# Four S5 pairs side by side: the lag matrices of a hybrid trunk in four column quarters of TensorE

## The chip, the cores and the metric

The kernel runs on one core of one Trainium2 chip. The metric is device time in microseconds (us). Three runs of the kernel before gave 1427.63, 1430.24 and 1431.34 us, median 1430.24.

A core has five engines that work side by side, each through its own list of instructions in order: TensorE (PE in the profile, its weight loads apart as PEld), VectorE (DVE), ScalarE (ACT), GpSimd (POOL) and SyncE (SP). They wait for each other by semaphores. DMAs are issued from the lists of SP, ACT and POOL. A TensorE product holds one operand still (the weights, up to 128 rows by 128 columns) and moves the other through; the columns of the weights become the partitions of the result, in an accumulator (PSUM). What takes a product of fp32 operands is two records in the trace.

## The reference

Four layers over 256 time steps of width 1024, all fp32. Each adds a mixer, an MLP and an embedding gate to `h`; the mixer of layers 0 and 3 is S5, a diagonal complex state-space layer over 64 groups of 16 channels with 64 states each:

```
def s5_mixer(xn, w_in, lam_re, lam_im, log_dt, b_re, b_im, c_re, c_im, d_skip, w_glu, w_out):
    u = (xn @ w_in).astype(f32)
    dt = jnp.exp(log_dt.astype(f32))[:, None]
    mag = jnp.exp(lr * dt)
    ab_re, ab_im = mag * jnp.cos(li * dt), mag * jnp.sin(li * dt)
    ...
    bbar_re = coef_re[..., None] * br - coef_im[..., None] * bi
    bbar_im = coef_re[..., None] * bi + coef_im[..., None] * br
    ...
        x_re = jnp.einsum('bsgc,gnc->bsgn', u_blk, bbar_re)
        x_im = jnp.einsum('bsgc,gnc->bsgn', u_blk, bbar_im)
        pa_re, pa_im, s_re, s_im = lax.associative_scan(_cplx_combine, (a_re, a_im, x_re, x_im), axis=1)
    ...
        y = jnp.einsum('bsgn,gcn->bsgc', s_re, cr) - jnp.einsum('bsgn,gcn->bsgc', s_im, ci)
    ...
    y = y.swapaxes(0, 1).reshape(bsz, t, D_MODEL) + d_skip.astype(f32) * u
    z = jax.nn.gelu(y).astype(xn.dtype) @ w_glu
    z1, z2 = jnp.split(z, 2, axis=-1)
    return (z1 * jax.nn.sigmoid(z2)) @ w_out

def reference(...):
    for i in range(DEPTH):                       # mixers: S5, FoX, GLA, S5
        h = h + mixer(rmsnorm(h, norm_mix[i]))
        h = h + sqrelu_mlp(rmsnorm(h, norm_mlp[i]), mlp_w1[i], mlp_w2[i])
        gate = jax.nn.sigmoid(rmsnorm(h, norm_ple[i]) @ ple_gate[i])
        h = h + (p[i] @ ple_proj[i]) * gate
    return rmsnorm(h, final_norm)
```

FoX (layer 1) is an attention with forget gates, GLA (layer 2) a gated linear attention.

## The kernel before

**Dense products.** Weights come from HBM in units of 512 KB (`raw`) on SP's queue. ACT rounds each unit (L179, `whi`), DVE makes the rest (L181, `wlo`), and TensorE multiplies high by high, high by low and low by high (L198 to L200, or in wider pieces L234 and L236). The stages outside S5 are almost wholly such products.

**S5 in steps of four.** Time is cut into 64 chunks of four steps. For the 64 steps of the chunk index a scan carries the state; within a chunk of four an input acts on an output 0 to 3 steps later by a small matrix of 16 by 16 channels, the lag matrix (the skip `d` is added to lag 0). The 64 groups go in 32 pairs, and the pairs in four blocks `b` of eight. For a block:

- `U` (L984): the block's inputs, loaded from DRAM by eight DMAs, alternately on ACT and SP.
- the way in, `s5_way_in` (L996): `U` times `wh`/`wl` (the matrices B with their powers) into `wk`, 64 products.
- rotation, scan and turning back on DVE (L908 to L911, L1006 to L1011, L1021 to L1025), which give `R`, `P` and `W`.
- `s5_way_out` (L926 to L938): `qo` (C with the powers of the state matrix, DVE) and `bx` (B masked by group, ACT).
- `s5_inside` (L942 to L954), the lag matrices. For each pair and each of real and imaginary part one product: weights `bx`, 128 rows by 32 columns (two groups of 16 channels); moving `qo`, 64 columns (four lags by 16 channels). The result of a block, `pk`, is 32 partitions by 8 pairs by 64. It stands in one accumulator bank (tag `mk`, one buffer), which an opening product with zeros (L946) sets up; a closing product of the identity with `dd` (`d` on the diagonals, L951) adds the skip. ACT copies it to `kk` (L953).
- `s5_lags` (L956 to L964): four DMAs (L961) write `kk` into `tm`, 128 partitions (32 channels by four input steps), shifted by 16 columns for each step, so that `tm` holds all lags of a chunk. In layer 0 they go from `kk` on ACT and SP, two on each.
- `s5_outputs` (L1042): `U` times `tm`, then `P` and `W` times `qo`, into a bank of the same tag `mk`; Gelu (L1051); transposition (L1058).

**Layer 3 is prepared ahead.** What of S5 does not depend on `h` is made for layer 3 by a generator, `s5_ahead`, whose steps are put between the dense products of earlier layers: `win`, `rot`, `qo` and `kk` of each block are stored in DRAM (`kept`; `kk` in slot 3) by DMAs on POOL, and read back in layer 3 on POOL's queue, `kk` by four shifted DMAs into `tm`. So of layer 3's four lag blocks only the reading stands in layer 3; their products stand in dense stages.

**What sets the order.** In layer 0 a string of steps (a letter and a block) gives the order in which the program is written:

```
FIRST = """i0 w2 w3 r0 x0 f2 w4 o0 j2 P0 s0 k0 w5 u1 w6 d0 e0 y0 r1 i1 f3 x1 t0 o1 j3 k1 g0 u2 w7 l0 P1 d1 s1 a0 p0 e1 y1 r2 i2 x2 t1 o2 k2 g1 ...
```

(`w` in-projection, `u` loads of `U`, `x` way in, `o` way out, `k` lag products, `s` and `e` scan and turning, `y` outputs, `t` and `g` transposition and split, `d` and `l` loads and splits of the next weights, `a` and `b` gate products, `p` embedding product.) A scheduler then orders each engine's list by its own estimate of times, and gives semaphores and buffers; it may move an instruction past others of its engine. A change of an instruction's kind can thus move others.

## Time and profile before

| | us |
|---|---|
| three runs, median | 1430.24 |
| profiled execution, span from first to last instruction | 1426.6 |
| PE busy in it | 1396.1 |
| PE weight loads (beside PE) | 1258.1 |
| DVE busy | 1034.8 |
| ACT busy | 710.6 |
| POOL busy | 100.6 |
| mean DMA rate | 178 GB/s |

The profile gives of the profiled execution no time but its span; the median of the three runs is 3.6 us above it. A line such as

```profile
L949 PE MATMUL mk<-qo,bx x256: 219/219/311, 37.6 to 1046.2; 128*32 128x64 f32 x128
```

reads: line 949 of the program, on PE, result `mk` from `qo` (moving) and `bx` (weights), 256 records, the shortest, median and longest in ns, the first and last start in us; then weights 128 rows by 32 columns and 128 partitions by 64 moving elements. The ends of matmuls are modelled and overlap the next one's start, so what a product costs is read from start to start. "idle before <-" names the time in which the engine had nothing to do before an instruction and what it waited for. The granted clock, 1.00 where nothing is throttled, was 0.996 in the mean.

Of the eight lag blocks four lie in layer 0 (at 37.6, 61.3, 80 to 86 and 110.7 us of the span) and four in dense stages, ahead for layer 3 (at 606, 892, 951 and 1042 us).

### The profile page before, as it was taken

The page shows a single profiled execution, that of the slowest core. Times are in us where ns is not written, and L with a number is a line of the kernel's source. Part 1 is how long each engine was busy: PE and PEld are TensorE (multiplying, and loading weights), DVE is VectorE, ACT ScalarE, POOL GpSimd, SP SyncE. Part 2 cuts the span into 40 slices and gives each one's busy share as a digit, 9 for nine tenths or more (in the row PEclk, how much of TensorE's full clock was granted, in tenths as well). Part 3 has the DMA queues.
Part 4 walks back from the last instruction along what each step waited for, and adds up shares of the span by engine and source line. Part 5 has one row for each costly group of instructions (what it writes and reads, how often), then busy time and mean ns, then how long its engine had stood idle before and what let it go on. Part 6 is the DMA issues. An engine that isn't in the chain of part 4 may idle for free.

```text
span 1426.6 us, 26530 instructions
## 1 busy us (share of the span) xinstructions
PE 1396.1 (98%) x10754; PEld 1258.1 (88%) x10754; DVE 1034.8 (73%) x1636; ACT 710.6 (50%) x1110; POOL 100.6 (7%) x167
## 2 busy tenths in 40 slices
PE   9999999999999999999999999999999999999997
PEld 8889988889999888889989588888998899888897
DVE  9985678776866678897676468878656946766765
ACT  3234465454655665455567445445552345545543
POOL 3000000010110000100005000000003100000020
PEclk9999999999999999999999999999999999999999
DMA  9443556657554355866565445667656556556661
GB/s 299 113 121 110 184 170 196 190 180 237 178 150 137 120 167 186 270 210 201 193 181 152 133 129 183 207 195 221 201 188 196 185 183 179 178 176 205 187 184 60
DMA packets 143227, 254.54 MB, mean 178 GB/s; under 512 B 21648, under 2 KB 32240, under 8 KB 143104
## 3 DMA queue, kind: packets, MB, share of 16 engines
q1 hardware_dynamic: 129856, 227.66, 51.8%
q0 software_dynamic: 7360, 23.73, 4.8%
q10 hardware_dynamic: 5888, 1.44, 0.5%
q8 instruction: 84, 1.38, 0.4%
q14 instruction: 39, 0.32, 0.1%
HBM read 242.15 MB, written 7.86 MB: 175 GB/s over the span
## 4 chain that ended last, share of the span: by engine, by line
PE 66%; DVE 1%; ACT 1%; issue 1%; DMA 0%; DVEq 0%; POOLq 0%; ACTq 0%
PE wk L234 9%; PE acc L234 7%; PE wk L236 4%; PE wk L198 4%; PE wk L200 4%; PE wk L199 4%; PE acc L236 4%; PE acc L198 3%; PE acc L199 3%; PE acc L200 3%; PE mk L234 3%; PE po L234 2%; PE acc L1150 1%; PE mk L236 1%; PE acc L259 1%; PE acc L258 1%
## 5 line engine op out<-in xcount | busy, mean ns | idle before, releaser
L181 DVE TENSOR_TENSOR wlo<-raw,whi 128x1024 fp32r<-128x1024 f32 x396 | 482.2, 1226 | 278.3 <-ACT whi L179 275.6
L179 ACT CAST whi<-raw 128x1024 fp32r<-128x1024 f32 x396 | 412.2, 1049 | 461.2 <-DMA raw<-mlp_w 69.1
L234 PE MATMUL wk<-x,whi 128*128 128x512 f32 x576 | 181.3, 396 | 1.1 <-DVE relu L245 1.1
L236 PEld LDWEIGHTS wk<-x,wlo 128*128 128x128 f32 x576 | 106.8, 188 | 23.4
L234 PE MATMUL acc<-s,whi 128*128 128x512 f32 x384 | 119.2, 395 | 0.0
L236 PE MATMUL wk<-x,wlo 128*128 128x256 f32 x576 | 112.9, 279 | 0.0
L234 PEld LDWEIGHTS wk<-x,whi 128*128 128x128 f32 x576 | 90.3, 189 | 3.6 <-DVE relu L245 1.4
L236 PEld LDWEIGHTS acc<-s,wlo 128*128 128x128 f32 x384 | 71.0, 188 | 16.1
L198 PE MATMUL acc<-x,whi 128*128 128x256 f32 x288 | 81.7, 287 | 0.8 <-ACT pp L432 0.8
L200 PE MATMUL acc<-x,wlo 128*128 128x256 f32 x288 | 82.2, 286 | 0.2 <-DVE wlo L181 0.2
L199 PE MATMUL acc<-x,whi 128*128 128x256 f32 x288 | 81.8, 285 | 0.0
L234 PE MATMUL mk<-x,whi 128*128 128x512 f32 x256 | 81.7, 396 | 0.0
L236 PE MATMUL acc<-s,wlo 128*128 128x256 f32 x384 | 75.4, 280 | 0.0
L200 PE MATMUL wk<-s,wlo 128*128 128x256 f32 x256 | 72.4, 283 | 0.0
L199 PE MATMUL wk<-s,whi 128*128 128x256 f32 x256 | 72.4, 283 | 0.0
L198 PE MATMUL wk<-s,whi 128*128 128x256 f32 x256 | 72.4, 283 | 0.0
L234 PE MATMUL po<-s,whi 128*128 128x512 f32 x192 | 60.3, 395 | 0.0
L234 PEld LDWEIGHTS acc<-s,whi 128*128 128x128 f32 x384 | 59.1, 188 | 0.9
L234 PE MATMUL wk<-s,whi 128*128 128x512 f32 x192 | 59.1, 395 | 0.0
L234 PE MATMUL acc<-x,whi 128*128 128x512 f32 x192 | 58.8, 396 | 0.0
L236 PEld LDWEIGHTS mk<-x,wlo 128*128 128x128 f32 x256 | 47.6, 188 | 10.3
L198 PEld LDWEIGHTS acc<-x,whi 128*128 128x128 f32 x288 | 54.8, 191 | 2.1 <-ACT pp L432 1.3
(405 smaller groups left out, 3405.7 us busy)
## 6 DMA issues: line engine op xcount, KB each, us to landing
raw<-mlp_w SPq DMA_DIRECT2D x256, 512.0 KB, 4.1
raw<-s_w_glu SPq DMA_DIRECT2D x32, 512.0 KB, 4.1
raw<-ple_gate SPq DMA_DIRECT2D x32, 512.0 KB, 3.8
raw<-fox_w_in SPq DMA_DIRECT2D x24, 512.0 KB, 3.9
raw<-gla_w_in SPq DMA_DIRECT2D x24, 512.0 KB, 4.4
raw<-s_w_out SPq DMA_DIRECT2D x16, 512.0 KB, 3.7
kept<-kept POOLq DMA_DIRECT2D x12, 512.0 KB, 5.6
raw<-ple_proj SPq DMA_DIRECT2D x8, 512.0 KB
```

Of the source, the lines that this page charges most:

```text
L179: nc.scalar.copy(hi, raw)
L181: self.last_lo = nc.vector.tensor_tensor(lo, raw, hi.bitcast(F32), ALU.subtract)
L198: mm(ps, hi, x[:, 0], start=first, stop=False, skip_group_check=True)
L199: mm(ps, hi, x[:, 1], start=False, stop=False, skip_group_check=True)
L200: self.last_mm = mm(ps, lo, x[:, 0], start=False, stop=last, skip_group_check=True)
L234: mm(ps[n], hi[:, i, s], v[i], start=first and i == 0, stop=False, skip_group_check=True)
L236: self.last_mm = mm(ps[n][:, 0], lo[:, i, s], v[i][:, 0], start=False, stop=last and i == UK - 1, skip_group_check=True)
L258: mm(ps[half], a[:, 0, t], hi[:, k], start=k0 + k == 0, stop=False)
L259: mm(ps[half], a[:, 0, t], lo[:, k], start=False, stop=False)
L1150: self.last_mm = nc.tensor.matmul(ps[:, n], raw[:, k, c], x[4 * i + k], start=i == k == n == 0, stop=i == 1 and k == 3, skip_group_check=True)
```

## The change

The sixteen products of a block keep their size, but are laid out in four column quarters: pair `p = 2 r + h` goes to columns 32 r to 32 r + 31, so to partitions 32 r to 32 r + 31 of the result, which is now 128 partitions by two pairs by 64. The four quarters follow each other in the order of the program; the first product of each quarter opens it (`start`), and the product with zeros is gone. The skip is added by four products of the identity, 32 columns each, one for each quarter; `dd` becomes 128 by 8 by 16 for 32 by 32 by 16, and for it `eye16` gets 128 rows (three additions for one) and the skip's table another layout, made on the host. `kk` is 128 by 128 for 32 by 512.

`s5_lags` wants the eight pairs of a channel in one partition. So `kk` now goes to DRAM first, by four DMAs, one a quarter: in layer 0 into a new `lags`, alternately on ACT and SP, and from there by the four shifted DMAs into `tm`; for layer 3 into `kept` as before, by four DMAs on POOL for one.

```diff
--- before.py
+++ after.py
@@ -99,8 +99,11 @@
         nc.gpsimd.affine_select(self.blk[:, 1:2], self.ones[:, :1], [[0, 1]], ALU.is_ge, 0.0, base=-64, channel_multiplier=1)
         self.nblk = const("nblk", [P, 2])
         nc.scalar.mul(self.nblk, self.blk, -1.0)
-        self.eye16 = const("eye16", [32, 16])
-        nc.vector.tensor_tensor(self.eye16, self.ident[0:32, 0:16], self.ident[0:32, 16:32], ALU.add)
+        self.eye16 = const("eye16", [P, 16])
+        eyes = const("eyes", [P, 64])
+        nc.vector.tensor_tensor(eyes, self.ident[:, 0:64], self.ident[:, 64:128], ALU.add)
+        nc.vector.tensor_tensor(eyes[:, 0:32], eyes[:, 0:32], eyes[:, 32:64], ALU.add)
+        nc.vector.tensor_tensor(self.eye16, eyes[:, 0:16], eyes[:, 16:32], ALU.add)
         self.zero = const("zero", [1, 512], BF16)
         nc.gpsimd.memset(self.zero, 0.0)
         self.halfpi = const("halfpi", [P, 1])
@@ -715,7 +718,7 @@
         lam = self.lam if self.lam is not None else self.s5_load(j)
         self.lam = None
         lr, li, ld = (lam[:, i, :] for i in range(3))
-        sd = self.small("sd", [32, 32], bufs=1)
+        sd = self.small("sd", [128, 8], bufs=1)
         (nc.sync if late else nc.gpsimd).dma_start(sd, self.A["s5_dT"][j])
         new = lambda name: self.small(name, [128, 32], bufs=1)
         tt = V.tensor_tensor
@@ -818,8 +821,8 @@
         cmul(at(F8, 3, 5), at(F8, 1, 3), rep(F8, 2, 2), 32, 2)
         yield
         cmul(at(F8, 5, 8), at(F8, 1, 4), rep(F8, 4, 3), 32, 3)
-        d = self.small("dd", [32, 32, 16], bufs=1)
-        self.tc.keep_in_program_order(V.tensor_tensor(d, self.eye16.unsqueeze(1).broadcast_to([32, 32, 16]), sd.unsqueeze(2).broadcast_to([32, 32, 16]), ALU.mult))
+        d = self.small("dd", [128, 8, 16], bufs=1)
+        self.tc.keep_in_program_order(V.tensor_tensor(d, self.eye16.unsqueeze(1).broadcast_to([128, 8, 16]), sd.unsqueeze(2).broadcast_to([128, 8, 16]), ALU.mult))
         r4 = new("r4")
         tt(r4, mag, mag, ALU.mult)
         tt(r4, r4, r4, ALU.mult)
@@ -936,22 +939,31 @@
         for g in range(2):
             nc.scalar.activation(bx[:, 0, :, g, :], bc[:, 0], AF.Identity, scale=self.blk[:, g:g + 1])
             nc.scalar.activation(bx[:, 1, :, g, :], bc[:, 1], AF.Identity, scale=self.nblk[:, g:g + 1])
-        dd = q["d"][:, ps]
+        dd = q["d"][:, 2 * b:2 * b + 2]
         return out, qo, bx, dd
 
     def s5_inside(self, b, out, qo, bx, dd, ahead=False):
 
         nc = self.nc
-        pk = self.psum((32, 8, 4, 16), "mk")
-        nc.tensor.matmul(pk, self.zero[:, 0:32], self.zero, start=True, stop=False, skip_group_check=True)
-        for p in range(8):
+        pk = self.psum((128, 2, 4, 16), "mk")
+        rows = [slice(32 * r, 32 * r + 32) for r in range(4)]
+        for h in range(2):
             for i in range(2):
-                nc.tensor.matmul(pk[:, p], bx[:, i, p].rearrange("x g c -> x (g c)"), qo[i][:, 0:4, p, :],
-                                 start=False, stop=False, skip_group_check=True)
-        nc.tensor.matmul(pk[:, :, 0, :], self.ident[0:32, 0:32], dd, start=False, stop=True, skip_group_check=True)
-        kk = self.t2("kk", (32, 8, 4, 16))
-        nc.scalar.copy(kk, pk)
-        return out, self.keep(b, 3, kk, ahead) if ahead else self.s5_lags(b, kk.rearrange("x p l c -> x p (l c)"), (nc.scalar, nc.sync))
+                for r in range(4):
+                    p = 2 * r + h
+                    nc.tensor.matmul(pk[rows[r], h], bx[:, i, p].rearrange("x g c -> x (g c)"), qo[i][:, 0:4, p, :],
+                                     start=h == i == 0, stop=False, skip_group_check=True)
+        for r in range(4):
+            nc.tensor.matmul(pk[rows[r], :, 0, :], self.ident[rows[r], rows[r]], dd[rows[r]], start=False, stop=True, skip_group_check=True)
+        kk = self.t2("kk", (128, 2, 64))
+        nc.scalar.copy(kk, pk.rearrange("x h l c -> x h (l c)"))
+        if not ahead and b == 0:
+            self.lags = self.dram.tile([4, 32, 512], F32, name="lags")
+        to = self.kept[0][b, 3, 0:32, 0:512] if ahead else self.lags[b]
+        for r in range(4):
+            queue = nc.gpsimd if ahead else (nc.scalar, nc.sync)[r % 2]
+            queue.dma_start(to[:, r * 128:(r + 1) * 128], kk[rows[r]].rearrange("x h e -> x (h e)"))
+        return out, kk if ahead else self.s5_lags(b, to.rearrange("x (p f) -> x p f", p=8), (nc.scalar, nc.sync))
 
     def s5_lags(self, b, kk, queues):
 
@@ -1418,7 +1430,7 @@
     o["s5_lam"] = np.stack([state(a["s5_lam_re"]), state(a["s5_lam_im"]), state(ldt)], axis=2)
     b = lambda v: v.reshape(n, 4, 8, 2, 64, 16).transpose(0, 3, 4, 1, 2, 5).reshape(n, 128, 4, 8, 16)
     c = lambda v: v.reshape(n, 4, 8, 2, 16, 64).transpose(0, 3, 5, 1, 2, 4).reshape(n, 128, 4, 8, 16)
-    o["s5_dT"] = a["s5_d"].reshape(n, 32, 32).transpose(0, 2, 1)
+    o["s5_dT"] = a["s5_d"].reshape(n, 4, 4, 2, 32).transpose(0, 2, 4, 1, 3).reshape(n, 128, 8)
 
     bT = lambda v: np.broadcast_to(v.reshape(n, 4, 8, 2, 64, 16).transpose(0, 1, 3, 5, 2, 4)[:, :, :, :, None], (n, 4, 2, 16, 4, 8, 64)).reshape(n, 4, 128, 512)
     o["s5_bT"] = np.stack([bT(a["s5_b_re"]), bT(a["s5_b_im"])], axis=3)
```

The names of lines below are those of each program (the change moves them by 3 to 12).

**ACT's list, around the lag matrix of block 1 in layer 0** (`kk` is the copied result, `U` the next block's inputs, `tm_...` the lag matrices, `whi` a rounded weight unit). Before:

```order
L953 COPY kk<-mk 32x512
L179 CAST whi<-raw 128x1024
L961 DMA tm_109<-kk 32x512
L961 DMA tm_109<-kk 32x8x32
L984 DMA U<-u 128x1x64 x4
```

Now:

```order
L959 COPY kk<-mk 128x128
L965 DMA lags<-kk 32x128 x2
L996 DMA U<-u 128x1x64
L973 DMA tm_112<-lags 32x512
L973 DMA tm_112<-lags 32x8x32
L996 DMA U<-u 128x1x64 x3
```

The rounding of a weight unit has moved ahead, out of this place; two writes to `lags` have come in, and three of the four `U` loads stand behind the reads into `tm`, one ahead of them. On SP the loads of `U` are parted in the same way, and three weight loads now stand ahead of that block's writes.

**PE's list, around the outputs of block 0 in layer 0** (`U` with `tm_...`, then `P` and `W`, are the outputs; `wk<-U` is the way in of block 1). Before:

```order
L1150 MATMUL acc<-x,wh 128x256 x7
L1042 MATMUL mk<-tm_108,U 64x64 x16
L1042 MATMUL mk<-qo,P 64x64 x32
L1042 MATMUL mk<-qo,W 64x64 x32
L996 MATMUL wk<-U,wh 64x64 x2
```

Now:

```order
L1162 MATMUL acc<-x,wh 128x256 x8
L1054 MATMUL mk<-tm_111,U 64x64 x16
L1008 MATMUL wk<-U,wh 64x64 x2
L1008 MATMUL wk<-U,wl 64x64 x2
L1008 MATMUL wk<-U,wh 64x64 x2
L1008 MATMUL wk<-U,wl 64x64 x2
L1008 MATMUL wk<-U,wh 64x64 x2
L1008 MATMUL wk<-U,wl 64x64
L1054 MATMUL mk<-qo,P 64x64 x32
L1054 MATMUL mk<-qo,W 64x64 x32
L1008 MATMUL wk<-U,wl 64x64
```

Eleven way-in products of block 1 have moved ahead of the products with `P`. In the next block, 24 of block 2's 64 way-in products have moved ahead of the products with `tm`.

**DVE's list, around `qo` of block 2 in layer 0** (`qo` and `scratch` are the two halves of a complex product, which the subtraction and the addition of `qo<-qo,scratch` join, here with the numbers that tell block 2's (1085, now 1101) from block 3's (1429, now 1451); `wlo` is the rest of a weight unit; `F` are powers). Before:

```order
L911 TENSOR_TENSOR rot_999<-rot_999,scratch_1000 128x8x64
L926 TENSOR_TENSOR scratch_1086<-bc_550,cpow_252 128x1280
L181 TENSOR_TENSOR wlo_1316<-raw_1154,whi_1315 128x1024
L926 TENSOR_TENSOR qo_1429<-bc_814,cpow_252 128x1280
L929 TENSOR_TENSOR qo_1085<-qo_1085,scratch_1086 128x640
L930 TENSOR_TENSOR qo_1085<-qo_1085,scratch_1086 128x640
L908 TENSOR_TENSOR scratch_1344<-F1_312,F8_313 128x1024
```

Now:

```order
L914 TENSOR_TENSOR rot_1015<-rot_1015,scratch_1016 128x8x64
L184 TENSOR_TENSOR wlo_1338<-raw_1176,whi_1337 128x1024
L929 TENSOR_TENSOR scratch_1102<-bc_553,cpow_255 128x1280
L932 TENSOR_TENSOR qo_1101<-qo_1101,scratch_1102 128x640
L933 TENSOR_TENSOR qo_1101<-qo_1101,scratch_1102 128x640
L911 TENSOR_TENSOR scratch_1366<-F1_315,F8_316 128x1024
L929 TENSOR_TENSOR qo_1451<-bc_824,cpow_255 128x1280
```

The rest of the weight unit stands ahead of the multiplication into `scratch`, and block 3's multiplication has moved behind the two joins.

## The prediction

> **What bounds the kernel now.** I read the page's busy shares first, then the chain of waits, then busy time by stretch.
>
> ```profile
> span 1426.6 us, 26530 instructions
> PE 1396.1 (98%) x10754; PEld 1258.1 (88%) x10754; DVE 1034.8 (73%) x1636; ACT 710.6 (50%) x1110; POOL 100.6 (7%) x167
> PE 66%; DVE 1%; ACT 1%; issue 1%; DMA 0%; DVEq 0%; POOLq 0%; ACTq 0%
> ```
>
> PE is busy 98% of the span and makes nearly all of the chain that is named. A microsecond of TensorE work saved is a microsecond of time where PE runs without a gap, and is nothing where it then waits. So the stretch decides:
>
> ```profile
> 28.00:55.00 27.00, 24.99 (x330) 21.82 (x330) 26.77 (x32) 5.26 (x12) 4.21 (x8) 1.00 0.62 179
> 55.00:80.00 25.00, 23.67 (x564) 21.95 (x560) 18.97 (x22) 8.50 (x16) 0.54 (x1) 1.00 0.27 73
> 80.00:100.00 20.00, 17.76 (x164) 15.59 (x165) 18.88 (x24) 4.84 (x10) 0.21 (x2) 0.91 0.29 79
> 600.00:620.00 20.00, 20.00 (x136) 17.13 (x136) 17.11 (x23) 11.94 (x21) 1.08 (x2) 1.00 0.70 227
> 1040.00:1080.00 40.00, 40.00 (x315) 38.14 (x315) 22.46 (x34) 21.62 (x38) 2.96 (x4) 1.00 0.54 179
> ```
>
> (Stretch, length, then busy us of PE, weight loads, DVE, ACT, POOL; granted clock, DMA share, GB/s.) The lag products of the last layer are made ahead, one block in each of four dense stages: there PE has no gap. In layer 0 the first 55 us belong to DVE (26.77 of 27.00), and PE waits at a few places:
>
> ```profile
> PE mk L1042 <- DVE P L1021: 2.0, 1, 2.0
> PE acc L198 <- DVE u L1156: 1.5, 2, 1.2
> PE mk L949 <- DVE qo L929: 1.4, 1, 1.4
> ```
>
> **The products, in the dense stages.** One block in PE's timeline:
>
> ```profile
> 606.30 0.39 PE L946 MATMUL mk<-zero 1*32 1x512 bf16 x1
> 606.62 1.97 PE L949 MATMUL mk<-qo,bx 128*32 128x64 f32 x32
> 608.52 0.40 PE L951 MATMUL mk<-dd,ident 32*32 32x128 f32 x2
> 608.85 0.73 PE L234 MATMUL acc<-x,whi 128*128 128x512 f32 x2
> ```
>
> From start to start: zero product 0.32, sixteen products (32 records) 1.90, identity 0.33; together 2.55. The 1.90 is 59 ns a record. What four tiles side by side cost is not in the trace; two side by side are:
>
> ```profile
> 20.88 2.09 PE L852 MATMUL wk<-ct,pick 128*64 128x64 f32 x64
> 22.89 3.72 PE L1150 MATMUL acc<-x,wl 128*128 128x256 f32 x16
> ```
>
> These have the same 64 moving columns and full 128 rows, but alternate between two column halves: 64 records in 2.01, 31 ns each, half of 59. Bounds for four quarters: 31 (two overlap, a third does not) and 15 (all four). I take 24, above the middle, since only two are shown. [...]
>
> So 32 x 0.024 = 0.77 for 1.90. The zero product goes, its 0.32 with it. Four identity products of 32 columns replace one of 128; the same elements in more, shorter pieces: I leave 0.33 (0.2 if they overlap, 0.5 if each drains). Saving: 1.13 + 0.32 = 1.45 a block, bounds 1.07 to 1.88. Four blocks of the last layer: **5.8 us** (4.3 to 7.5). Nothing there hides it: PE is 20.00 of 20.00 busy, and DVE, which feeds it, has 2.9 of those 20 us spare.
>
> What else this part adds: three more DMA issues a block on POOL. The last block is the one that could hurt, as POOL's power step for the next norm stands behind it:
>
> ```profile
> 1072.04 0.55 POOL L976 DMA_DIRECT2D kept<-kk  x1 [16.50 <-ACT kk L953]
> 1079.31 0.71 POOL L341 TENSOR_TENSOR rrow<-rrow,mhalf 128x2 f32<-128x2 f32 x1 [6.72 <-DVE rrow L337]
> ```
>
> 3 x 0.55 = 1.65 us more against 6.72 idle: nothing; without that cover, 1.65. The blocks are read back only later, in the last layer.
>
> **Layer 0, what it gains.** Block 0's products save 1.45 in DVE's stretch, so nothing. But DVE saves there itself: `dd` now has 128 elements a partition for 512.
>
> ```profile
> 19.13 0.67 DVE L822 TENSOR_TENSOR dd<-eye,sd 32x512 f32<-32x512 f32 x1
> 14.63 0.29 DVE L701 TENSOR_TENSOR F<-F 128x128 f32<-128x128 f32 x1
> 6.41 0.19 DVE L748 TENSOR_TENSOR cs<-sh 128x32 f32<-128x32 f32 x1 [0.99 <-ACT sh L740]
> ```
>
> That is 0.67 - 0.29 = 0.38. The two additions for the taller `eye` (some 0.1 each by starts) lie ahead of a wait of 0.99 for ACT and vanish in it. Then PE's wait of 2.0 for `P` is filled with eleven of the next block's 64 way-in products, each 64 columns on 64 rows and two records (the fence on PE's order). Block 3's products of that shape, quoted below, start at 119.89 and 120.87: 32 records in 0.98, 0.061 for a product of two; 11 x 0.061 = 0.67.
>
> Blocks 1 to 3 save 3 x 1.45 = 4.35 of PE work. Block 2 has more in it:
>
> ```profile
> 78.41 1.23 DVE L181 TENSOR_TENSOR wlo<-raw,whi 128x1024 fp32r<-128x1024 f32 x1 [2.86 <-ACT whi L179]
> 79.55 1.48 DVE L926 TENSOR_TENSOR qo<-bc,cpow 128x1280 f32<-128x1280 f32 x1
> 81.83 0.30 PE L949 MATMUL mk<-qo,bx 128*32 128x64 f32 x2 [1.45 <-DVE qo L929]
> 82.56 3.21 PE L949 MATMUL mk<-qo,bx 128*32 128x64 f32 x30 [0.44 <-DVE qo L930]
> 85.70 0.63 PE L951 MATMUL mk<-dd,ident 32*32 32x128 f32 x2
> ```
>
> DVE is late with `qo` because a weight split that waits 2.86 and the next block's multiplication of 1.48 stand ahead of it; in the new order the load of that split's unit stands on SP ahead of block 1's writes to `lags`, and the multiplication comes after. The two waits (1.89) should go. After them the 30 records took 3.14 where 30 x 0.059 = 1.78 is normal: the clock was down (0.91 in that stretch), 1.36 more. Together 3.2; I count 1.8, since the steps that follow hang on DVE's scan, which moves up less.
>
> **Layer 0, what it pays.** `tm` now comes by way of DRAM. Block 3, where nothing else stands between:
>
> ```profile
> 112.90 0.40 PE L951 MATMUL mk<-dd,ident 32*32 32x128 f32 x2
> 114.19 0.56 ACT L953 COPY kk<-mk 32x512 f32<-32x512 f32 x1
> 114.78 1.19 ACTq L961 DMA_DIRECT2D tm<-kk  x2
> 119.89 1.15 PE L1042 MATMUL mk<-tm,U 64*64 64x64 f32 x32
> 120.87 2.03 PE L1042 MATMUL mk<-qo,P 64*64 64x64 f32 x64
> tm<-kk ACTq DMA_DIRECT2D x4, 64.0 KB, 2.0
> tm<-kk ACTq DMA_DIRECT2D x4, 32.0 KB, 3.0
> U<-u ACTq DMA_DIRECT2D x32, 32.0 KB, 2.5
> tm<-kept POOLq DMA_DIRECT2D x4, 64.0 KB, 5.7
> tm<-kept POOLq DMA_DIRECT2D x4, 16.0 KB, 4.7
> ```
>
> Now `tm` is there at 114.78 + 0.6 + 3.0 = 118.4, and PE reads it at 119.89: 1.5 spare. The hop costs an issue (0.6) and a landing, between 2.0 (the copy without DRAM) and 5.7 (the slowest read from it); the shorter `kk` and its place ahead of the last `bx` give back 0.55. Late by 0.55 to 4.25; I take 1.0, with a landing near the 2.5 of `U`, whose 32 KB are the nearest in size to the 16 KB of each piece of `lags`. Blocks 1 and 2 come out alike (1.0 each), and in block 1 half of `U` is now issued behind `tm`, on ACT and SP both, while 24 way-in products that need it are put ahead of the step that reads `tm`: 0.7 more. Sum 3.7, bounds 1.5 and 13. Block 0 has ten microseconds of products between, and covers the hop.
>
> That third weight load ahead of block 1's writes on SP has a risk of its own:
>
> ```profile
> 70.34 1.22 DVE L181 TENSOR_TENSOR wlo<-raw,whi 128x1024 fp32r<-128x1024 f32 x1
> 70.47 1.15 PE L1042 MATMUL mk<-tm,U 64*64 64x64 f32 x32
> ```
>
> Its buffer is freed by the split at 70.34. If that split stayed there, the writes behind it would leave at 71.6, `tm` would be there after two issues and two landings (0.6 + 2.5 + 0.6 + 3.0) at 78.3, and block 1's step, at 70.47, would be 7.8 late. The rounding ahead of that chain has moved up on ACT's list, out of its place beside `kk`, so I count the load as in time; the 7.8 stays within the bound of 13. Behind the waiting ACT queue stand the `U` loads, the copy `pp` and a weight split; on SP the `U` loads and the next weight load.
>
> Layer 0: 0.38 + 0.67 + 4.35 + 1.8 - 3.7 = **3.5 us** gained (bounds: 8 gained, 7 lost).
>
> **The sum.** 5.8 + 3.5 = 9.3: the span of 1426.6 would be 1417.3. The runs' median, 1430.24, is 3.6 above that span, which I keep: 1420.9, say **1421**.
>
> **Rivals.**
> - *Only the dense stages gain.* Layer 0's stalls eat its savings, as DVE sets the pace there: for it, 26.77 of 27.00 and the three waits on DVE; against it, PE was busy 23.67 of 25 after that by the same view. Time 1430.2 - 5.8 + 1 = 1425.
> - *The quarters do not overlap.* [...] As a mechanism here, every record would stay at 59 ns: only the zero product goes, 4 x 0.32 = 1.3 in the dense stages and 1.0 in layer 0, against 3.7 of stalls and some 1 us of shorter waits: 1430. Against it stand the 31 ns above, also with full rows.
> - *The DRAM hop decides.* With a landing of 5.7 on the write as on the read, each of blocks 1 to 3 waits 4.25, and block 0 about 2 at PE's wait for `P`; DVE and both queues then stand as well. 3 x 4.25 + 2 = 15, less 5.8 and 3.5 of PE work that still counts: 5.7 slower, 1436. It decides from a landing of about 4.5. For it: reads back from DRAM in this program do take 4.7 to 5.7 on POOL's queue; against it, these go through ACT's and SP's.
> - *More than forecast.* 15 ns a record (1.88 a block) and all of block 2's 3.2: 7.5 + 6.5 = 14: 1416.
>
> **How the numbers follow.** Chances: forecast 0.45, only the dense stages 0.25, more than forecast 0.10, no overlap 0.10, DRAM hop 0.10. 0.3% (4.3 us) is about what a measurement of this kernel tells from no change, so faster means under 1426. The first and the third are faster; the second lies at that edge, six in ten on the faster side: 0.70 faster; its rest and no overlap: 0.20 same; the hop 0.10 slower. The range leaves out the hop and the ends of the others: 1412 to 1431; the forecast's own is 1416 to 1426.
>
> **What would show it.** In PE's timeline a dense block's sixteen products in 0.5 to 1.0 us, no zero product, the whole in about 1.1: the first term. 1.9 again: no overlap. In layer 0, idle time of PE before the step that reads `tm`, put down to a DMA: each over 2 us makes the hop the cause. No wait of L949's successor for `qo` in block 2: the third term. I am wrong if the time after layer 0 and the time from there to the end do not move by about 3.5 and 5.8.

## The result, and the profile after

The changed kernel took 1418.35 us in the median of six runs (1417.02 to 1422.11), the kernel before 1430.62 (six runs, 1427.63 to 1432.34). The ratio is 0.9916, 95% interval 0.9902 to 0.9929: 12.3 us faster, where 9.3 was forecast. A run's time is 1.7 to 2.0 above its span (1417.53 for the profiled execution, whose span is 1415.8). By the two profiled spans the gain is 10.8; the profiled execution of before, some 1426.6 + 1.7, lay 2.3 below that kernel's median, the one after 0.8 below its own. The terms of the prediction were counted on spans, so it is the 10.8 that they are compared with below.

First the page's head, and the same dense block as before the change in PE's timeline:

```profile
span 1415.8 us, 26660 instructions
PE 1384.2 (98%) x10794; PEld 1248.7 (88%) x10794; DVE 1034.0 (73%) x1638; ACT 707.8 (50%) x1110; POOL 106.6 (8%) x179
...
603.70 0.66 PE L954 MATMUL mk<-qo,bx 128*32 128x64 f32 x32
604.29 0.26 PE L957 MATMUL mk<-dd,ident 32*32 32x32 f32 x8
604.48 0.73 PE L237 MATMUL acc<-x,whi 128*128 128x512 f32 x2
```

From start to start the sixteen products take 0.59, or 18 ns a record for 59; the four identity products 0.19 for 0.33; together 0.78 for 2.55. Four blocks in the dense stages save 4 x 1.77 = 7.1.

To part layer 0 from the rest I use the first product of layer 0's MLP, the first start of this group (before, then after):

```profile
L234 PE MATMUL mk<-x,whi x256: 387/395/499, 179.7 to 1347.3; 128*128 128x512 f32 x128
...
L237 PE MATMUL mk<-x,whi x256: 387/395/404, 176.6 to 1335.5; 128*128 128x512 f32 x128
```

It stands at 179.7 before and 176.6 after: layer 0's mixer gives 3.1. From there to the end it takes 1426.6 - 179.7 = 1246.9 and 1415.8 - 176.6 = 1239.2: the rest gives 7.7.

What PE waits for in layer 0 now (engine, line, waited for: total us, times, longest):

```profile
PE acc L202 <- DVE g L1234: 2.7, 2, 1.9
PE mk L1054 <- DVE P L1033: 1.9, 1, 1.9
PE mk L1054 <- DMA tm<-lags: 1.4, 1, 1.4
```

The waits of block 2 for `qo` (1.45 and 0.44) are gone; a wait of 1.4 for `tm` in block 1 and one of 1.9 for the split of `g` in block 3 have come. Block 2's lag products have another wait in their middle, for which the profile shows no releaser ("issue"); with it they take 1.46 and not 0.59:

```profile
79.12 0.47 PE L954 MATMUL mk<-qo,bx 128*32 128x64 f32 x17
80.22 0.43 PE L954 MATMUL mk<-qo,bx 128*32 128x64 f32 x15 [0.64 <-issue]
```

One more thing has come with the waits. This is PE's granted clock around the wait for `P` and around the wait for `g`, and last the one such place of layer 0 before the change, in stretches of 3.41 us, as long as the clock stood at 0.50 each time (stretch, length, busy us of PE, weight loads, DVE, ACT, POOL; granted clock, DMA share, GB/s):

```profile
48.95:52.36 3.41, 1.50 (x52) 1.36 (x47) 3.41 (x8) 0.00 (x0) 0.00 (x0) 1.00 0.83 220
52.36:55.77 3.41, 3.41 (x64) 3.41 (x66) 2.22 (x3) 1.62 (x2) 0.00 (x0) 0.50 0.09 32
55.77:59.18 3.41, 3.41 (x122) 3.41 (x120) 1.96 (x2) 1.97 (x4) 0.00 (x0) 1.00 0.41 131
...
106.98:110.39 3.41, 1.30 (x8) 1.10 (x9) 3.41 (x5) 1.50 (x6) 0.00 (x0) 1.00 0.34 92
110.39:113.80 3.41, 3.41 (x18) 3.41 (x17) 3.41 (x7) 0.00 (x0) 0.00 (x0) 0.50 0.27 96
...
79.43:82.84 3.41, 1.52 (x14) 0.90 (x13) 3.38 (x5) 0.79 (x2) 0.00 (x0) 1.00 0.45 153
82.84:86.25 3.41, 3.41 (x31) 2.87 (x28) 3.41 (x5) 0.44 (x2) 0.00 (x0) 0.50 0.02 5
```

After a stretch in which PE was idle for 1.9 to 2.1 of 3.41 us, the next 3.41 us ran at half the clock, 0.50 for 1.00 (called a half-rate stretch below), which by an estimate, half of 3.41, costs 1.7 where PE is the bound. Layer 0 has two such stretches after the change and had one before (at 82.84, after the waits for `qo`).

So the dense stages answer to the forecast, and layer 0 gives nearly the size forecast (3.1 for 3.5). Whether for the reasons forecast, the experiments had to tell.

### The profile page after: what moved, and what is told of

It reads as the page before. It is cut to its first block, busy times and chain, and to the rows that moved or that the text cites. A ratio compares the mean times of both kernels' runs of the same rounds, so it can differ in the third digit from the quotient of the medians.

```text
span 1415.8 us, 26660 instructions
## 1 busy us (share of the span) xinstructions
PE 1384.2 (98%) x10794; PEld 1248.7 (88%) x10794; DVE 1034.0 (73%) x1638; ACT 707.8 (50%) x1110; POOL 106.6 (8%) x179
## 4 chain that ended last, share of the span: by engine, by line
PE 64%; DVE 2%; ACT 1%; DMA 1%; issue 0%; SPq 0%; DVEq 0%; POOLq 0%; ACTq 0%
PE wk L237 9%; PE acc L237 7%; PE wk L239 4%; PE wk L201 4%; PE wk L203 4%; PE wk L202 4%; PE acc L239 3%; PE acc L201 3%; PE acc L202 3%; PE acc L203 3%; PE mk L237 3%; PE po L237 2%; PE mk L239 1%; PE acc L262 1%; PE acc L261 1%; PE acc L263 1%
```

## The experiments

All twelve kernels compute the whole program. Four theories stood against each other for layer 0's 3.1: the new products themselves; the smaller skip table; a hop through DRAM that takes a part back; and the order that the scheduler made of layer 0, which differs from the kernel before at more places than the edit names.

**How products share the array (one_quarter, two_quarters).** The order of the sixteen products alone is changed.

```diff
-        for h in range(2):
-            for i in range(2):
-                for r in range(4):
+        for r in range(4):              # two_quarters: for r0 in (0, 2), h, i, r in (r0, r0 + 1)
+            for h in range(2):
+                for i in range(2):
```

> The changed kernel, but its sixteen products in the order of the quarters: four in quarter 0, four in quarter 1 and so on, so that neighbours share a quarter except at three places. Theory (products overlap only where neighbours stand in different quarters): 32 records at 59 ns each but for three changes of quarter, 1.7 to 1.9 us a block for 0.59. Rival (the shorter result, 32 partitions by 128 elements in one bank without the zero product, makes them fast, in whatever order): 0.6 a block.

> The changed kernel, but the sixteen products alternate between quarters 0 and 1 first and between 2 and 3 then. One quarter at a time took 1.32 for 32 records, four in turn 0.59. Theory (the time of a record is shared by the quarters that alternate): 30 ns a record, 0.95 to 1.0 a block. Rival (what counts is only that a neighbour differs): 18 to 20 ns as with four, 0.6.

PE's timeline of layer 0's first block, of the one and of the other:

```profile
37.99 1.39 PE L954 MATMUL mk<-qo,bx 128*32 128x64 f32 x32
39.32 0.26 PE L957 MATMUL mk<-dd,ident 32*32 32x32 f32 x8
```

```profile
37.11 0.90 PE L955 MATMUL mk<-qo,bx 128*32 128x64 f32 x32
37.95 0.26 PE L958 MATMUL mk<-dd,ident 32*32 32x32 f32 x8
```

Start to start 1.33, 0.84 and, with four in turn, 0.59: 42, 26 and 18 ns a record in the mean. The more quarters alternate, the less a record costs, so products of different quarters do overlap here, each with the full 128 rows.

The timeline joins the records; taken singly, their starts in the traces' first dense block say more. Before the change each record starts 56 ns after the one before it. With two quarters in turn two records start within 7 ns and the next two 56 ns after them (four where the second two quarters begin, which makes the mean 26); with four in turn four start within 20 ns and the next four 56 ns after. So a quarter starts a record every 56 ns, and quarters run side by side: the theory of two_quarters holds. (The means of 59 and 18 have some 0.1 us for the end of the block in them: from the last record to the first identity product it is some 150 ns in each of these kernels.)

One quarter at a time took 42, not the 59 of before and not the 1.7 to 1.9 us expected, because a change of quarter saves more than one record. In one_quarter's dense block the records that take 243 ns and not 219, one for each quarter and the first of each by the order of the program, start at 605.53, 605.78, 606.04 and 606.29: each quarter begins 0.25 us after the one before, beside its fifth record of eight, and not behind its eighth. So three records overlap at each of three changes, which leaves 23 of 32, and 23 x 56 ns = 1.29. (Which quarter a record belongs to is read from this pattern; the trace does not name it.) Why the next quarter can begin there and not earlier isn't shown. By one run each, these kernels took 1422.68 and 1421.17 us.

**The two parts apart, first try (ahead_only, layer0_only).** The new products in the dense stages alone, and in layer 0 alone. Both keep the old skip table beside the new one, in an input of its own.

```diff
+        self.eye_old = const("eye_old", [32, 16])
+        nc.vector.tensor_tensor(self.eye_old, self.ident[0:32, 0:16], self.ident[0:32, 16:32], ALU.add)
...
-            outs[b] = self.s5_inside(b, *outs[b])
+            outs[b] = self.s5_inside_old(b, *outs[b])       # ahead_only; in layer0_only the two calls of s5_ahead
```

> The four blocks of the dense stages as in the changed kernel, layer 0's four as before. Theory (the two parts add): the first MLP product stays at 179.6 us as before, and from there to the end it takes 1239.3 as in the changed kernel, for 1247.0: span 1418.9, 7.7 less than before, ratio 0.9946. Four blocks at 0.78 for 2.55 give 7.1 of it. Rival (dense stages give only what their products save by the prediction, 5.8, and layer 0 the rest of the 10.8): span 1420.8, ratio 0.996.

> Layer 0's four blocks as in the changed kernel, the dense stages' four as before. Theory (adding): the first MLP product at 176.5, 3.1 earlier than before, the rest unchanged: span 1423.5, ratio 0.9978, which lies at the edge of what can be measured. Rival (layer 0 gains nothing of its own and only moves, its DRAM hop eating the products' 7.1): first MLP product at 179 to 180, ratio 1.000.

Measured: 1422.88 (ratio 0.9943, 0.9929 to 0.9956) and 1429.23 (0.9995, 0.9984 to 1.0005). Together that is 9.5 of 12.3 us. Both started late. The first `U` loads of layer 0 on ACT's queue, in ahead_only, in layer0_only and in the changed kernel:

```profile
23.53 9.39 ACTq L1014 DMA_DIRECT2D U<-u  x4
```

```profile
22.97 10.26 ACTq L1014 DMA_DIRECT2D U<-u  x4
```

```profile
22.71 3.97 ACTq L996 DMA_DIRECT2D U<-u  x4
```

Four small issues take 9 to 10 us for 4. Whether the further input did that or the executions differ there, I can't say; without that input 3.79 (before), 5.05 (dense_new) and 6.50 (four_copies) were seen. Layer 0's first lag products stand at 40.04 and 44.03 for 37.25. By block 1 ahead_only has made that up (61.98, and 61.61 before the change), layer0_only hasn't (64.50), so layer0_only says nothing on layer 0; ahead_only comes back behind the table below.

**The two parts apart, cleanly (dense_new, layer0_new).** One skip table, the new one; the old products take it by four products of the identity.

```diff
+    def s5_inside_old(self, b, out, qo, bx, dd, ahead=False):       # as before, but:
+        for r in range(4):
+            rows = slice(32 * r, 32 * r + 32)
+            nc.tensor.matmul(pk[:, 2 * r:2 * r + 2, 0, :], self.ident[:, rows], dd, start=False, stop=True, skip_group_check=True)
...
-            outs[b] = self.s5_inside(b, *outs[b])
+            outs[b] = self.s5_inside_old(b, *outs[b])       # dense_new; in layer0_new the two calls of s5_ahead
```

> Again the new products in the dense stages alone, now with one table and one layout of the skip (the new one, 128 by 8 by 16) and no further input; layer 0 has the old sixteen products with the zero product, its skip added by four products of the identity into 32 partitions, and kk without DRAM. The question is whether the two parts add, after the first pair of kernels (0.9943 and 0.9995, whose product is 0.9938 against 0.9916) lost time at their start. Theory (they add, and the missing 3 us were the slower issue of the first U loads, 9.4 and 10.3 us on ScalarE for 4.0): 4 blocks x 1.77 = 7.1 and VectorE's 0.4: ratio 0.995. Rival (the dense stages give more than their products save): 0.992 to 0.993.

> The counterpart: new products and the way through DRAM in layer 0 alone, the dense stages with the old products, one layout of the skip. Theory (adding): what is left of 12.3, 12.3 - 7.1 = 5.2: ratio 0.9964, first MLP product near 176.5. Rival (layer 0 gains nothing: what its products save turns into waits for VectorE and for tm): ratio 0.999 to 1.000, first MLP product at 179 to 180.

Measured: 1419.0, ratio 0.9911 (0.9897 to 0.9924), and 1426.02, ratio 0.9964 (0.9953 to 0.9976). layer0_new came out as its theory of adding had it (0.9964), dense_new lower than both of its forecasts. The dense stages' products alone give as much as the whole change, and layer 0's alone give 5 us: the parts do not add. The first MLP product of dense_new and of layer0_new:

```profile
L237 PE MATMUL mk<-x,whi x256: 387/395/404, 174.7 to 1333.8; 128*128 128x512 f32 x128
```

```profile
L237 PE MATMUL mk<-x,whi x256: 387/395/404, 176.6 to 1343.1; 128*128 128x512 f32 x128
```

In dense_new layer 0 has the old products, the zero product and `kk` without DRAM, and yet ends at 174.7, 5.0 earlier than before and 1.9 earlier than in the changed kernel. So something other than the products moved layer 0. VectorE's list shows it; this is dense_new around the place where the split had waited 2.86 at 78.41:

```profile
72.95 1.23 DVE L184 TENSOR_TENSOR wlo<-raw,whi 128x1024 fp32r<-128x1024 f32 x1 [0.38 <-ACT whi L182]
74.09 1.48 DVE L929 TENSOR_TENSOR scratch<-bc,cpow 128x1280 f32<-128x1280 f32 x1
75.49 1.48 DVE L929 TENSOR_TENSOR qo<-bc,cpow 128x1280 f32<-128x1280 f32 x1
76.89 0.81 DVE L932 TENSOR_TENSOR qo<-qo,scratch 128x640 f32<-128x640 f32 x1
```

The split is done 5.5 us earlier, and `qo` behind it 4.1 earlier, though block 3's multiplication still stands ahead of the join. Before the change this join stood here:

```profile
80.95 0.82 DVE L929 TENSOR_TENSOR qo<-qo,scratch 128x640 f32<-128x640 f32 x1
```

What is earlier is the split's weight unit. The rounding of the first and of the third unit of that chain and the loads of SP, before, and then after:

```profile
60.82 1.05 ACT L179 CAST whi<-raw 128x1024 fp32r<-128x1024 f32 x1 [2.38 <-PE wk L996]
71.59 8.45 SPq L171 DMA_DIRECT2D raw<-s_w_glu  x2
77.33 1.04 ACT L179 CAST whi<-raw 128x1024 fp32r<-128x1024 f32 x1 [5.04 <-DMA raw<-s_w_glu]
```

```profile
54.13 1.04 ACT L182 CAST whi<-raw 128x1024 fp32r<-128x1024 f32 x1 [14.66 <-DMA raw<-s_w_glu]
49.11 14.66 SPq L174 DMA_DIRECT2D raw<-s_w_glu  x3
71.75 1.05 ACT L182 CAST whi<-raw 128x1024 fp32r<-128x1024 f32 x1
```

Three units go one after the other through rounding and split. Before, the first waited on ACT for the way-in products (60.82), and the third was issued behind the `U` loads, at 71.59 at the earliest. Now the first is rounded at 54.13, and the third unit stands on SP ahead of block 1's writes to `lags`.

**The load alone (dense_late, after_late, old_early).** The next two kernels put the third unit back to where it was before the change, once with old and once with new products in layer 0:

```diff
...
-            units[i % 2, i // 2] = self.raw(w_glu...)
+            with self.tc.issue_after(self.u_loads[2].ins) if first and i == 3 else nullcontext():
+                units[i % 2, i // 2] = self.raw(w_glu...)
```

> The kernel with the new products in the dense stages alone (0.9911, first MLP product at 174.7 for 179.7 before, though layer 0 has the old products), with one edit: the third weight unit of layer 0's gate is issued on SyncE behind the U loads of block 2, as in the kernel before, for ahead of block 1's tm. Theory (layer 0's gain is a matter of that load: its unit's split is then not late, and block 2's qo behind it on VectorE): the split waits for its unit again until about 78, block 2's lag products wait for qo, and the first MLP product goes back to 178 to 180: ratio 0.9945. Rival (another difference of layer 0's order made it faster): stays at 0.991 to 0.992.

> The changed kernel with the same edit: the third weight unit of layer 0's gate behind block 1's U loads on SyncE. Theory (the new products give layer 0 nothing, the earlier load gave it all): the first MLP product at 178 to 180 for 176.6, ratio 0.994 to 0.995, that is what the dense stages save and no more. Rival (the new products give layer 0 its 3 to 5 us themselves): 0.9916 stays.

(`u_loads[2]` is the last of block 2's `U` loads on SP; the lines that note it are left out here.) And old_early has the old products everywhere (dense_new with the two calls of `s5_ahead` changed too); on SP its order of layer 0 is that of dense_new:

> Old products everywhere, with the zero product and kk without DRAM; the only differences from the kernel before are the new layout of the skip (added by four products of the identity, 128 rows) and the scheduler's order of layer 0, which is that of the kernel with new products in the dense stages alone: the third weight unit is issued on SyncE ahead of block 1's tm. Theory (the earlier load gives layer 0 its 3 to 5 us, whatever the products are): first MLP product at 174 to 176 for 179.7, from there to the end as before, ratio 0.9965 to 0.998. Rival (layer 0 gains by the new products of the dense stages' kernel in some other way, or the load saves only the 2.0 that the medians of the two kernels with new dense products show, 0.9911 and 0.9924): ratio 0.9985 or more.

Measured: dense_late 1420.98 (0.9924, 0.9911 to 0.9936), after_late 1422.33 (0.9944, 0.9930 to 0.9958), old_early 1423.35 (0.9943, 0.9929 to 0.9956). Their first MLP products, in this order:

```profile
L238 PE MATMUL mk<-x,whi x256: 387/395/404, 179.2 to 1338.2; 128*128 128x512 f32 x128
```

```profile
L238 PE MATMUL mk<-x,whi x256: 387/395/404, 180.8 to 1339.2; 128*128 128x512 f32 x128
```

```profile
L237 PE MATMUL mk<-x,whi x256: 387/395/497, 174.8 to 1342.3; 128*128 128x512 f32 x128
```

and the split that waits again, in dense_late and in after_late:

```profile
79.00 1.23 DVE L185 TENSOR_TENSOR wlo<-raw,whi 128x1024 fp32r<-128x1024 f32 x1 [3.10 <-ACT whi L183]
```

```profile
76.16 1.23 DVE L185 TENSOR_TENSOR wlo<-raw,whi 128x1024 fp32r<-128x1024 f32 x1 [2.26 <-ACT whi L183]
```

With these the cases fill a table (us; the spans of dense_new, layer0_new, dense_late, after_late and old_early are 1414.1, 1422.7, 1418.5, 1419.5 and 1421.5):

| kernel | products in layer 0 | in the dense stages | third unit | first MLP product | from there to the end | median |
|---|---|---|---|---|---|---|
| before | old | old | late | 179.7 | 1246.9 | 1430.62 |
| old_early | old | old | early | 174.8 | 1246.7 | 1423.35 |
| dense_late | old | new | late | 179.2 | 1239.3 | 1420.98 |
| dense_new | old | new | early | 174.7 | 1239.4 | 1419.0 |
| layer0_new | new | old | early | 176.6 | 1246.1 | 1426.02 |
| after_late | new | new | late | 180.8 | 1238.7 | 1422.33 |
| after | new | new | early | 176.6 | 1239.2 | 1418.35 |

By the traces the three causes are plain. New products in the dense stages: 7.4 less from the first MLP product to the end, whatever layer 0 does (1239.2 in the mean for 1246.6). The early unit: 4.9, 4.5 and 4.2 less in layer 0, whatever the products are. The last two come from kernels that differ in this one edit; the first, from before to old_early, has the whole new order in it. New products in layer 0, with their way through DRAM: 1.6 to 1.9 *more* in layer 0.

Half-rate stretches are part of these numbers. In layer 0 there are one in before, dense_late and layer0_new, two in after, three in after_late, none in dense_new and old_early. At 1.7 each, the new products would without them be worth between 1.8 less and 0.1 more, and the early unit 2.5 to 3.2 less. In before the stretch follows the late unit's waits; in dense_late it stands at 53.5, ahead of the late split, so there it is not the unit's doing.

The smaller skip table is in dense_late too, beside the old products and the late unit, and layer 0 ends 0.5 earlier there than before the change; by these traces it gives no more. ahead_only is a further case of new dense products with the late unit: SP issues the unit at 71.94 at the earliest, its split waits 2.72, and layer 0 ends at 180.7, with two half-rate stretches for dense_late's one. Over all fourteen traces the stretch from the first MLP product to the end takes 1238.7 to 1243.8 with the new dense products in any order and 1246.1 to 1249.3 with the old ones.

The medians scatter more, as executions of one kernel differ by 3 to 6 us, but agree in the mean over their pairs: dense 4.4, 7.7 and 9.6 less (mean 7.2); early 2.0, 4.0 and 7.3 less (4.4); layer 0's products 2.7 and 1.4 more and 0.7 less (1.1 more).

**The way through DRAM (four_copies, two_hops).** Four copies on ACT shift the quarters back to 32 partitions, so that neither layer's products need DRAM to regroup; and, on the other side, the way through DRAM twice.

```diff
-        kk = self.t2("kk", (128, 2, 64))
-        nc.scalar.copy(kk, pk.rearrange("x h l c -> x h (l c)"))
...
+        kk = self.t2("kk", (32, 8, 64))
+        for r in range(4):
+            nc.scalar.copy(kk[:, 2 * r:2 * r + 2], pk[rows[r]].rearrange("x h l c -> x h (l c)"))
```

```diff
+        if not ahead:
+            if b == 0:
+                self.lags2 = self.dram.tile([4, 32, 512], F32, name="lags2")
+            for r in range(2):
+                (nc.scalar, nc.sync)[r].dma_start(self.lags2[b][16 * r:16 * r + 16], to[16 * r:16 * r + 16])
+            to = self.lags2[b]
```

> The changed kernel with its quarters, but the regrouping without DRAM in both layers: four copies on ScalarE, each from one quarter's 32 partitions to partitions 0 to 31, give the old kk of 32 by 512; layer 0's four DMAs go from it into tm directly, the kept copy is one DMA again. Theory 1 (the hop through DRAM is on layer 0's path): the wait of 1.45 for tm in block 1 goes, tm comes some 4 us earlier in each block, and the first MLP product stands at 173.5 to 175: span 1413 to 1414.5. Rival (VectorE's scan and its split of g set the pace of layer 0, the hop lies beside them): the wait for tm goes and comes back as a wait for VectorE; first MLP product at 176 to 177, span 1415 to 1417.

> The changed kernel with the way through DRAM twice in layer 0: lags is copied to a second table there (two DMAs of half a block) before the four reads into tm. Theory 1 (the hop is on layer 0's path in blocks 1 to 3): some 3.5 to 4 us later for each tm; the wait of 1.45 in block 1 becomes 5, blocks 2 and 3, which now have 0.2 and about 1 us in hand, wait 3 each: 9 to 10 us more, ratio 0.998. Rival (PE waits for VectorE's P or g soon after in any case, which takes most of it up): 2 to 4 us more, ratio 0.993 to 0.9945.

four_copies: 1419.5 (0.9920, 0.9907 to 0.9932), first MLP product at 175.7, 0.9 earlier; two_hops: 1427.7 (0.9978, 0.9956 to 1.0001), at 183.5. PE's waits of the first at block 1, and of the second at blocks 1, 2 and 3:

```profile
66.67 1.15 PE L1049 MATMUL mk<-tm,U 64*64 64x64 f32 x32 [0.41 <-DMA tm<-kk]
68.13 2.08 PE L1049 MATMUL mk<-qo,P 64*64 64x64 f32 x64 [0.31 <-DVE P L1028]
```

```profile
73.90 0.33 PE L1014 MATMUL wk<-U,wh 64*64 64x64 f32 x4 [3.05 <-DMA U<-u]
98.39 1.15 PE L1060 MATMUL mk<-tm,U 64*64 64x64 f32 x32 [1.58 <-DMA tm<-lags]
123.69 1.15 PE L1060 MATMUL mk<-tm,U 64*64 64x64 f32 x32 [1.62 <-DMA tm<-lags]
```

Without DRAM the step that reads `tm` stands at 66.67 for 71.39, 4.7 earlier; 2.3 of that are there already at block 1's lag products (59.17 for 61.50), where four_copies, unlike the changed kernel, has no half-rate stretch in block 0. But layer 0 ends only 0.9 earlier: VectorE takes it up (waits of 1.26, 0.34 and 1.64 for `P`, `W` and `u` in block 2). So leaving out the first hop is worth hardly anything in the end, as its rival had it, though not purely: the scheduler's order of layer 0 is another again in four_copies (the third unit behind block 2's `U` loads, and its split behind the joins of `qo`), so the price of the hop alone stays open.

A second hop is not free: 9.3 us by the medians and 6.9 at the first MLP product. (Layer 0 began 2.1 later in that execution, but had made it up by block 1's lag products, at 60.08 for 61.50.) The sum is near what was forecast for a hop on the path, its places are not: PE's waits for `tm` came to 3.6 in all and not to 11, block 2's `U` loads cost 3.05, and the rest lies in other waits.

**The new wait for `g` (g_first).** VectorE joins `P` and `W` ahead of the split of `g` that PE waits for; here behind it.

```diff
+        with self.tc.issue_after(after.ins) if after else nullcontext():       # after: the split of g of the block before
             V.tensor_tensor(R[:, 0], X[:, :, 1], Y[:, :, 0], ALU.add)
             V.tensor_tensor(R[:, 1], X[:, :, 0], Y[:, :, 1], ALU.subtract)
...
```

> The changed kernel, with one edit on VectorE's list in layer 0: the two joins of P and W into R wait behind the split of g of the block before, which PE waits for (1.89 in block 3, 0.85 in block 1). Theory (VectorE sets the pace of layer 0 there, and the wait of 1.89 also brings the half-rate window that follows it, 1.7 lost): g comes 1.2 earlier, PE's wait falls to 0.7 and the window after it does not come: 1.2 to 3 us less than the changed kernel, 1415.4 to 1417, ratio 0.989 to 0.9905. Rival (the wait only moves on to the products that read P, as the scan is 0.7 later): as the changed kernel, 0.9916, within 0.001.

```profile
107.69 0.38 PE L202 MATMUL acc<-g,whi 128*128 128x256 f32 x1 [0.69 <-DVE g L1235]
...
114.94 1.15 PE L1055 MATMUL mk<-tm,U 64*64 64x64 f32 x32 [1.72 <-ACT whi L182]
```

In the trace the wait falls as expected, from 1.89 to 0.69, no half-rate stretch follows, and the first MLP product stands at 174.7, 1.9 earlier than in the changed kernel. But 1.3 of that are there already at block 1's lag products (60.19 for 61.50), since block 0's half-rate stretch is missing too, and a new wait of 1.72 stands at block 3's `tm`. The median is not lower: 1421.31, ratio 0.9938 (0.9924 to 0.9952), 3 us slower than the changed kernel. The profiled execution was the fastest of its five (1418.12); what the others lost isn't in a trace. I count it as inconclusive. No kernel tried is clearly faster than the changed one; dense_new, which leaves layer 0's products as they were, is as fast.

## Why the prediction was right, and where it was not

- **Dense stages, forecast 5.8, measured 7.4 to 7.7.** The mechanism was right: no gap on PE, the whole saving counts. The term was mis-sized: a record costs 18 ns, not 24, and the identity products take 0.19, not 0.33 (no trace had shown what the shorter pieces cost, so their 0.2 and 0.5 were estimates), so that a block saves 1.77, not 1.45; four make 7.1 of the 7.4 to 7.7. The bounds held (15 to 31 ns); without the block's end a record costs 14, a quarter of 56.
- **POOL's three further issues, forecast nothing.** Right; the last block's four issues are followed by 5.55 of waiting:

```profile
1062.41 2.03 POOL L965 DMA_DIRECT2D kept<-kk  x4 [16.19 <-ACT kk L959]
1069.99 0.71 POOL L344 TENSOR_TENSOR rrow<-rrow,mhalf 128x2 f32<-128x2 f32 x1 [5.55 <-DVE rrow L340]
```

- **Layer 0's products, forecast 4.35 for blocks 1 to 3.** This is the step that failed. Block 1's and block 3's saving came back as waits, for `tm` (1.45) and for `g` (1.89 for 0.46), and the latter brought a half-rate stretch (1.7); block 2's products had the wait of 0.64 in them whose cause stays open. I had quoted that VectorE sets the pace in the first 55 us, but counted PE's work in full after that. Old products with the early unit end layer 0 1.8 to 1.9 earlier than new ones.
- **Block 2's split, forecast 1.8.** Right in kind and too small: the earlier unit is worth 4.2 to 4.9 by the traces (2.5 to 3.2 without the half-rate stretches), against a gain of 3.1 in layer 0 as a whole. What I had taken off for the steps that hang on DVE's scan was not lost; the scan and `u` behind it moved up as well. It belongs to the scheduler's order, not to the products: old_early has it without any of them.
- **What layer 0 pays, forecast 3.7.** The step that reads `tm` waits for it 1.45 in block 1 and not in block 3; the 0.24 ahead of it in block 2 have no releaser in the profile. A kernel without DRAM, in another order, ends layer 0 only 0.9 earlier. The writes to `lags` landed 2.7 and 3.5 us after their issue, for the 2.5 assumed:

```profile
lags<-kk ACTq DMA_DIRECT2D x8, 16.0 KB, 3.5
lags<-kk SPq DMA_DIRECT2D x8, 16.0 KB, 2.7
```

  A second hop costs about what a hop on the path was to cost; the first, by these traces, lies for the most part beside VectorE's work. The risk of the third unit holding SP's writes did not come: the splits had moved up with the rounding, as argued.
- **0.38 and 0.67 in block 0.** `P` stands at 52.34 for 53.09, 0.75 earlier, but the half-rate stretch right behind it takes 1.5 back: block 0's transposition starts at 60.91 for 60.70.
- **Rivals.** That the quarters don't overlap is refuted by 18 ns against 59; that the DRAM hop decides, by the result and by four_copies. That only the dense stages gain is nearest to what the *products* do: dense_new, without new products in layer 0, is as fast as the whole change. It would have been the right account with the wrong time, since the order of layer 0 gave 3 to 5 us on its own.

So layer 0's 3.5 came out as 3.1 by luck, by errors that cancelled: 4.35 that was nothing, 1.8 that was 4.5, and 3.7 of stalls that were smaller but had half-rate stretches beside them. The dense stages' 7.7 for 5.8 is a size that was off, with its mechanism right.

## What to carry to other kernels

Small products with few weight columns are worth laying side by side in column quarters, in turn, where TensorE has no gap (here 18 ns a record for 59, and 7.4 us less behind layer 0's mixer); where another engine set the pace the saved time came back as waits (in layer 0 of 1.45 for `tm` and 1.89 for `g`). When a scheduler makes the order, compare the orders on the queues of weight loads before crediting an edit: here one load issued earlier gave about a third of the gain (4.4 of 12.3 us in the mean of the medians), and a kernel with old products and the new order shows it. Build the case "new order, old operation" whenever parts do not add.

## What the runs showed of the hardware

- The half-rate stretches lie on a fixed grid. In the traces of the changed kernel and of the one before, each of those up to 1395 us lasts 3.413 us at a clock of 0.50. In the changed kernel they begin at 52.36, 110.39 and 1090.0, the later two 17 and 304 times 3.413 us behind the first; in the kernel before at 82.84 and 1100.0, 298 times 3.413 us apart. With these two traces cut on their grids (25 to 1395 us), each of the 5 cuts in which PE was idle for 1.89 to 2.12 us was followed by a cut at half rate, and none of the 13 with 0.85 to 1.45 idle (the ends of PE's records are modelled, so the idle times are rough). A sharp bound isn't shown: in after_late one begins near 127.8, where the profile shows waits of 0.70 and 0.68 in the 3.4 us ahead of it. The kernel before waited 2.0 us at 51 us and kept its clock; that wait fell on two cuts, with 1.04 and 0.97 idle. So, with the 1.7 estimated above, a wait of 2 us cost 2 or 3.7 here, by where it fell.
- Up to 1395 us the kernel before has two such stretches and the changed kernel three; at 1.7 us each they are of the size by which executions of one kernel differ (5.1 us between the shortest and the longest of the changed kernel's six).
- Four small DMA issues (`U` on ACT's queue) took 3.79 (before), 3.97 (after), 3.99 (one_quarter), 5.05 (dense_new), 6.50 (four_copies), 9.39 (ahead_only) and 10.26 us (layer0_only) at the same place.
- The lag products, 128 rows by 32 columns with 64 columns moving, start 56 ns apart, a record, in one column quarter (before), and quarters run side by side: four in turn start four records in every 56 ns (after).
